# A decoder block on one core: the second channel product as seven block products on 2x2 blocks, left factors through DRAM

## The chip, the cores and the metric

The kernel runs on one core of a Trainium2 chip. A core has five engines that each work through their own instructions in order: TensorE (PE, matrix products into PSUM), VectorE (DVE), ScalarE (ACT), GpSimd (POOL) and SyncE (SP, which here only issues transfers). They wait for each other through semaphores. The metric is the device time of one execution in microseconds: 2101.83 us before the change, the median of three runs (2101.52 to 2101.94).

## The reference: what is computed

One decoder layer on 512 tokens of width 2048, all in float32: an input projection, eight heads of forgetting attention beside eight heads of spatial gating, an output projection with residual, and a channel MLP. The change is in the MLP and the norm behind it:

```
h2 = rmsnorm(x, norm_ffn_g)            # x: 512 x 2048
a = relu(h2 @ w_ff1)                   # first channel product, w_ff1: 2048 x 8192
x = x + (a * a) @ w_ff2                # second channel product, w_ff2: 8192 x 2048
return rmsnorm(x, norm_final_g)
```

## The kernel before, in words

Every large product is made of matmuls of 128x128 weights with 512 columns. To keep float32 accuracy each operand is split into two parts in the type fp32r (h = rounded, l = the rest), and `mm3` (L139) issues three matmuls: h by h, h by l and l by h.

The products are a list of units that `run_units` (L186) works through. A unit covers 512 output columns; each of its steps takes one weight tile of 128 rows by 512 columns and makes 12 matmuls on four PSUM banks. `prepare` (L190) runs three steps ahead: every second step it issues a load of two tiles (512 KB, `load_pair`, L156, on SP's queue), and `split_w` (L144) lets ACT make wh and DVE make wl, which are kept in four buffers of each.

The stream of the MLP goes in 16 parts of 512 hidden features. `f1_unit(u)` (L759) has 16 steps and makes part u of the first product, features on partitions, tokens on columns; `f1_done` (L617) scales by the norm's row rF and applies relu on DVE, squares on ACT, and splits the result into sh and sl, which stay in SBUF. `f2_unit(u)` (L762) follows one part behind: four units (g) of four steps, one for each 512 output columns, and `f2_done` (L629) adds the four banks into the running sum oa on DVE. So f and g alternate. The last part is `last_unit` (L639): by halves of 256 tokens, with matmuls of 256 columns (psl), and behind each half `last_norm` (L669) sums the squares, takes the root on POOL, spreads it over the partitions with a matmul and scales oa, which is stored to the output, features first.

The order on PE is the order of the program; the other engines' orders are made by a scheduler when the program is built. `tick` (L177) interleaves small tasks with the steps. PSUM has six banks for products (`mm`) and two more (`ax`).

## Time and profile before

| | |
|---|---|
| time, median of 3 runs | 2101.83 us |
| span of the profiled execution | 2100.5 us |
| time of a run outside such a span | about 1.3 us |
| PE busy | 2082.1 us (99%) |
| DVE busy | 1036.4 us (49%) |
| ACT busy | 740.7 us (35%) |
| POOL busy | 139.5 us (7%) |
| moved by DMA | 204.58 MB, mean 97 GB/s |

The page gives only the span of the profiled execution, from its first to its last instruction; what a run takes more than that is the difference of the first two rows. Busy time is the time in which an engine executes; a matmul's record is longer than the distance to the next, because matmuls are pipelined, so the pace is read from the starts. A wait that the page names with an arrow belongs to the engine that released it last.

### The profile page before, as it was taken

The numbers are of one execution on the slowest core, as the hardware profiler recorded it, in microseconds if no ns is written. First come the engines' busy times: TensorE is split into PE (matmuls) and PEld (weight loads), VectorE is DVE, ScalarE is ACT, GpSimd is POOL, SyncE is SP. The second block draws the span as 40 slices with busy tenths as digits, with TensorE's granted clock in tenths as the row PEclk, the third lists the DMA queues.
The fourth block names the chain that finished last, engine by engine and source line by source line (L and its number), as shares of the span: only waits on it lengthen the run. The fifth ranks groups of instructions, "written<-read, shape, count | busy, mean of one in ns | idle before, by whom it ended". The sixth has DMA issues, their size and how long they took to land.

```text
span 2100.5 us, 24282 instructions
## 1 busy us (share of the span) xinstructions
PE 2082.1 (99%) x9462; PEld 1728.6 (82%) x9462; DVE 1036.4 (49%) x1732; ACT 740.7 (35%) x1239; POOL 139.5 (7%) x123
## 2 busy tenths in 40 slices
PE   9999999999999999999999999999999999999997
PEld 6888888888888888888888888888888888888886
DVE  6466365575575644435334354343433434434465
...
DMA packets 60371, 204.58 MB, mean 97 GB/s; under 512 B 6496, under 2 KB 10720, under 8 KB 60128
## 3 DMA queue, kind: packets, MB, share of 16 engines
...
q8 instruction: 74, 1.21, 0.2%
...
q0 software_dynamic: 256, 0.52, 0.1%
...
## 4 chain that ended last, share of the span: by engine, by line
PE 97%; DVE 2%; issue 1%; ACT 0%; DMA 0%; SPq 0%; DVEq 0%; POOL 0%; ACTq 0%
PE ps_f L140 11%; PE ps_f L141 11%; PE ps_f L142 11%; PE ps_g L140 10%; PE ps_g L141 10%; PE ps_g L142 10%; PE ps_qk L140 3%; PE ps_qk L142 3%; PE ps_qk L141 3%; PE ps_zv L140 1%; PE ps_zv L142 1%; PE ps_zv L141 1%; PE ps_zu L142 1%; PE ps_zu L140 1%; PE ps_oa L141 1%; PE ps_oa L140 1%
## 5 line engine op out<-in xcount | busy, mean ns | idle before, releaser
L153 DVE SCALAR_TENSOR_TENSOR wl_f<-raw_f,cols,wh_f 128x512 fp32r<-128x512 f32 x256 | 193.1, 755 | 445.8 <-ACT wh_f L152 445.8
L140 PE MATMUL ps_f<-xh,wh_f 128*128 128x512 f32 x1024 | 398.5, 389 | 0.0
L142 PE MATMUL ps_f<-xh,wl_f 128*128 128x512 f32 x1024 | 398.4, 389 | 0.0
L141 PE MATMUL ps_f<-xl,wh_f 128*128 128x512 f32 x1024 | 398.4, 389 | 0.0
L140 PE MATMUL ps_g<-sh,wh_g 128*128 128x512 f32 x960 | 373.5, 389 | 0.0
L142 PE MATMUL ps_g<-sh,wl_g 128*128 128x512 f32 x960 | 373.5, 389 | 0.0
L141 PE MATMUL ps_g<-sl,wh_g 128*128 128x512 f32 x960 | 373.5, 389 | 0.0
L152 ACT ACTIVATE wh_f<-raw_f,cols 128x512 fp32r<-128x512 f32 x256 | 185.7, 726 | 494.4 <-PE ps_f L141 369.7
L149 DVE TENSOR_TENSOR wl_g<-raw_g,wh_g 128x512 fp32r<-128x512 f32 x240 | 165.4, 690 | 295.1 <-ACT wh_g L148 179.5
L148 ACT CAST wh_g<-raw_g 128x512 fp32r<-128x512 f32 x240 | 149.3, 622 | 405.8 <-PE ps_g L141 315.2
L140 PEld LDWEIGHTS ps_f<-xh,wh_f 128*128 128x128 f32 x1024 | 192.2, 188 | 39.9
L142 PEld LDWEIGHTS ps_f<-xh,wl_f 128*128 128x128 f32 x1024 | 192.2, 188 | 39.9
L141 PEld LDWEIGHTS ps_f<-xl,wh_f 128*128 128x128 f32 x1024 | 192.2, 188 | 39.9
L142 PEld LDWEIGHTS ps_g<-sh,wl_g 128*128 128x128 f32 x960 | 180.2, 188 | 37.4
L140 PEld LDWEIGHTS ps_g<-sh,wh_g 128*128 128x128 f32 x960 | 180.2, 188 | 37.4
L141 PEld LDWEIGHTS ps_g<-sl,wh_g 128*128 128x128 f32 x960 | 180.2, 188 | 37.4
L633 DVE TENSOR_TENSOR oa<-oa,ps_g 128x512 f32<-128x512 f32 x240 | 148.7, 680 | 7.4 <-PE ps_g L142 7.4
L140 PE MATMUL ps_qk<-xh,wh_qk 128*128 128x512 f32 x256 | 101.6, 397 | 0.0
L142 PE MATMUL ps_qk<-xh,wl_qk 128*128 128x512 f32 x256 | 100.0, 391 | 0.0
L141 PE MATMUL ps_qk<-xl,wh_qk 128*128 128x512 f32 x256 | 99.9, 390 | 0.0
L113 POOL TENSOR_TENSOR rt_last<-rt_last,neg_half 128x2 f32<-128x2 f32 x2 | 1.4, 697 | 1375.8 <-DVE rt_last L112 1375.8
L153 DVE SCALAR_TENSOR_TENSOR wl_qk<-raw_qk,cols,wh_qk 128x512 fp32r<-128x512 f32 x64 | 47.8, 750 | 69.8 <-ACT wh_qk L152 69.2
...
## 6 DMA issues: line engine op xcount, KB each, us to landing
raw_f<-in_w_dram SPq DMA_DIRECT2D x128, 512.0 KB, 3.5
raw_g<-in_w_dram SPq DMA_DIRECT2D x120, 512.0 KB, 3.5
raw_qk<-in_win_dram SPq DMA_DIRECT2D x32, 512.0 KB, 3.5
raw_zv<-in_win_dram SPq DMA_DIRECT2D x16, 512.0 KB, 3.5
raw_zu<-in_win_dram SPq DMA_DIRECT2D x16, 512.0 KB, 3.5
raw_oa<-in_wout_dram SPq DMA_DIRECT2D x16, 512.0 KB, 3.5
raw_og<-in_wout_dram SPq DMA_DIRECT2D x16, 512.0 KB, 3.5
raw_v<-in_win_dram SPq DMA_DIRECT2D x15, 512.0 KB, 3.5
```

The source lines that it names most:

```text
L113: nc.gpsimd.tensor_tensor(dst, dst, neg_half[:, 0:1].broadcast_to([P, m]), ALU.pow)
L140: nc.tensor.matmul(ps, lhsT=ah, rhs=bh, start=start, stop=False)
L141: nc.tensor.matmul(ps, lhsT=ah, rhs=bl, start=False, stop=False)
L142: nc.tensor.matmul(ps, lhsT=al, rhs=bh, start=False, stop=stop)
L148: nc.scalar.copy(wh, raw)
L149: nc.vector.tensor_tensor(wl, raw, f(wh), ALU.subtract)
L152: nc.scalar.activation(wh, raw, AF.Copy, scale=g)
L153: nc.vector.scalar_tensor_tensor(wl, raw, g, f(wh), ALU.mult, ALU.subtract)
L633: nc.vector.tensor_tensor(a, a, ps[m], ALU.add)
```

## The change

The second product no longer follows the first part by part: all 16 `f1_unit` run first, then `second_product` runs.

**Behind the output projection** the gain of the norm is put into xh and xl, so w_ff1 is only split (no gain), and the norm's scale is left out of the first product: its square r2, by token, is applied at the very end. `turn_x2` transposes the residual (64 transposes of 128x128) and stores it in DRAM as x2d.

**In the first product** `f1_done` makes relu and square on ACT. `factors_task` makes of each part's 512x512 result four blocks (two halves of the tokens, two halves of the hidden features) and of these seven left factors: A11, A12, A22 and the sums S1 to S4 (four POOL instructions). Each factor is split into h and l (7 casts on ACT, 7 subtractions on DVE) and stored in DRAM (`fac`, 3.67 MB for a part).

**In `second_product`** the output has tokens on partitions and stays in SBUF (acc). There are 16 units x = (kc, n): 1024 hidden features by 1024 output columns each. A unit takes four blocks B11, B12, B21, B22 of w_ff2, each in two pieces h of 256 rows, and makes seven products P1 to P7 in place of the eight that 2x2 blocks by 2x2 blocks take. A product and a piece h is a group of 12 matmuls: 14 groups a unit, 2688 matmuls in all. Right factors are B11, B21, B22 as they are, and three combinations made in place: raw(B11) = B12 - B11 and t2 = B22 - that on DVE (L739, L740), raw(B12) = B22 - B12 on POOL (L742), raw(B21) = B21 - t2 on DVE (L752). Each is split like before, now in pieces of 128x1024, by ACT (L749) and DVE (L750) into three buffers. The four output blocks of a unit are sums of products: some sums form in PSUM by further accumulation, and three times a unit (P2, P7, P3) `add_kept` adds the bank to acc on DVE and then, from the second kc on, a kept product s to acc on POOL (L783). In the last kc `settle` applies r2, adds x2d and squares; `finish` then makes the last norm for a half of the tokens, transposes back and stores.

```diff
+    dram = ctx.enter_context(tc.tile_pool(name="dram", bufs=1, space=bass.MemoryType.DRAM))
...
     def g_done(c):
...
-                nc.scalar.copy(xh[k], o)
-                nc.vector.tensor_tensor(xl[k], o, f(xh[k]), ALU.subtract)
+                nc.scalar.activation(xh[k], o, AF.Copy, scale=g)
+                nc.vector.scalar_tensor_tensor(xl[k], o, g, f(xh[k]), ALU.mult, ALU.subtract)
...
+            start_task(turn_x2(c), 6)
+    def turn_x2(c):
+        for m in range(4):
+            xt = t2(f"x2t{c}_{m}")
+            pt = ax(f"px{c}_{m}", m % 2)
+            for tb in range(NT):
+                nc.tensor.transpose(pt[:, tb * P:(tb + 1) * P], oa[c][:, m, tb * P:(tb + 1) * P], ident)
+            nc.scalar.copy(xt, pt)
+            nc.sync.dma_start(out=x2d[c][:, :, m * P:(m + 1) * P], in_=xt.rearrange("p (t c) -> p t c", c=P))
+            yield 2
     def norm2_task():
...
-        parts = spread_parts(r, "ffn")
-        yield 4
-        spread(rF, *parts, "ffn")
+        nc.vector.tensor_tensor(r2, r, r, ALU.mult)
...
-    def f1_done(u):
...
-    def f2_done(fb):
...
-    def last_unit():
...
-    def last_norm(half, squares, c, n):
...
-    def last_weights_task():
...
+    NF = 7
+    A11, A12, A22, S1, S2, S3, S4 = range(NF)
+    fac = [dram.tile([NF, P, 1024], F32, name=f"fac{u}") for u in range(NU)]
+    def f1_done(u):
+        def done(ps):
+            sq = s8(f"sq{u}")
+            for m in range(4):
+                nc.scalar.activation(sq[:, m, :], ps[m], AF.Relu)
+                nc.scalar.activation(sq[:, m, :], sq[:, m, :], AF.Square)
+            start_task(factors_task(u, sq))
+    def factors_task(u, sq):
+        def v(t):
+            return t.rearrange("p (j c) -> p j c", j=2)
+        a11, a21 = sq[:, 0:2, 0:256], sq[:, 0:2, 256:512]
+        a12, a22 = sq[:, 2:4, 0:256], sq[:, 2:4, 256:512]
+        s = s8(f"s{u}")
+        s1, s2, s3, s4 = (v(s[:, i, :]) for i in range(4))
+        form = [a11, a12, a22, s1, s2, s3, s4]
+        def put(i, n):
+            t = s8(f"fc{u}_{i}", F32R)
+            for k in range(n):
+                h, l = v(t[:, 2 * k, :]), v(t[:, 2 * k + 1, :])
+                nc.scalar.copy(h, form[i + k])
+                nc.vector.tensor_tensor(l, form[i + k], f(h), ALU.subtract)
+            nc.sync.dma_start(out=fac[u][i:i + n].rearrange("i p c -> p i c"),
+                              in_=f(t)[:, 0:2 * n, :].rearrange("p (i a) c -> p i (a c)", i=n))
+        nc.gpsimd.tensor_tensor(s1, a21, a22, ALU.add)
+        nc.gpsimd.tensor_tensor(s3, a11, a21, ALU.subtract)
+        yield 2
+        put(A11, 2)
+        yield 2
+        nc.gpsimd.tensor_tensor(s2, s1, a11, ALU.subtract)
+        nc.gpsimd.tensor_tensor(s4, a12, s2, ALU.subtract)
+        put(A22, 2)
+        yield 3
+        put(S2, 2)
+        yield 2
+        put(S4, 1)
+    def second_product():
...
+        y_pool = pool("y_pool", 6)
+        f_pool = pool("f_pool", NF)
+        raw2 = pool("raw2", 4)
+        tmp_pool = pool("tmp_pool", 1)
+        w2_pool = pool("w2_pool", 3)
...
+        P1, P2, P3, P4, P5, P6, P7 = range(1, 8)
+        left = {P1: A11, P2: A12, P3: S4, P4: A22, P5: S1, P6: S2, P7: S3}
+        usual = (P1, P2, P6, P5, P7, P3, P4)
+        final = (P1, P2, P5, P6, P3, P7, P4)
+        units2 = [(kc, n) for kc in range(NK) for n in range(2)]
...
+        def load_factor(kc, p):
+            if kc >= NK:
+                return
+            t = f_pool.tile([P, 2, 1024], F32R, tag="fac", name=f"fac{kc}_{p}")
+            for h in range(2):
+                nc.sync.dma_start(out=f(t)[:, h, :], in_=fac[2 * kc + h][left[p]])
+            facs[kc, p] = t
+        def prepare(i):
+            x, p, h = groups[i]
+            def raw(b):
+                return raws[x, b, h]
+            if (p == P6 and order_of(x) is usual) or (p == P5 and order_of(x) is final):
+                t2t = tmp_pool.tile([P, 1024], F32, tag=f"tmp{h}", name=f"tmp{x}_{h}")
+                nc.vector.tensor_tensor(raw(B11), raw(B12), raw(B11), ALU.subtract)
+                nc.vector.tensor_tensor(t2t, raw(B22), raw(B11), ALU.subtract)
+                raws[x, "t2", h] = t2t
+                nc.gpsimd.tensor_tensor(raw(B12), raw(B22), raw(B12), ALU.subtract)
+            src = {P1: B11, P2: B21, P3: B22, P4: B21, P5: B11, P6: "t2", P7: B12}[p]
+            s = raws[x, src, h]
+            wh = w2_pool.tile([P, 1024], F32R, tag="wh", name=f"wh{x}_{p}_{h}")
+            wl = w2_pool.tile([P, 1024], F32R, tag="wl", name=f"wl{x}_{p}_{h}")
+            nc.scalar.copy(wh, s)
+            nc.vector.tensor_tensor(wl, s, f(wh), ALU.subtract)
+            if p == P6:
+                nc.vector.tensor_tensor(raw(B21), raw(B21), raws[x, "t2", h], ALU.subtract)
+            ready[i] = wh, wl
+            freed = {P5: B11, P7: B12, P3: B22, P4: B21}.get(p)
+            if freed is not None:
+                nxt = {P5: B11, P7: B21, P3: B12, P4: B22}[p]
+                load(x + 1, nxt, h)
...
+        def add_kept(c, s, first, bank):
+            if first:
+                for t in range(2):
+                    nc.vector.tensor_tensor(acc[c][:, t, :], s[:, t, :], bank[t], ALU.add)
+            else:
+                take(bank, add_ps(c))
+                nc.gpsimd.tensor_tensor(acc[c], acc[c], s, ALU.add)
...
+        def settle(th, q, x2l):
+            a = acc[th, q]
+            for t in range(2):
+                tb = 2 * th + t
+                nc.vector.scalar_tensor_tensor(a[:, t, :], a[:, t, :], r2[:, tb:tb + 1], x2l[:, t, :],
+                                               ALU.mult, ALU.add)
+                nc.scalar.activation(x2l[:, t, :], a[:, t, :], AF.Square, accum_out=sums[:, tb, q:q + 1])
+
+        def finish(th):
+            tbs = slice(2 * th, 2 * th + 2)
+            r = rl[:, tbs]
+            nc.vector.tensor_reduce(r, sums[:, tbs, :], axis=AX.X, op=ALU.add)
+            inv_root(r, r, D, 2)
+            for q in range(4):
+                for t in range(2):
+                    e = nc.vector if t == 0 else nc.gpsimd
+                    e.tensor_scalar(acc[th, q][:, t, :], acc[th, q][:, t, :], rl[:, 2 * th + t:2 * th + t + 1], None, ALU.mult)
+            yield 3
...
+        for i, (x, p, h) in enumerate(groups):
+            while n_ready < len(groups) and n_ready <= i + 2:
+                prepare(n_ready)
+                n_ready += 1
+            kc, n = units2[x]
+            chain = {P1: "X", P6: "X", P7: "X", P4: "X", P2: "Y", P5: "Z", P3: "Z"}[p]
+            new = p in (P1, P2, P5)
+            if p == P4 and order_of(x) is final:
+                chain, new = "W", True
+            if h == 0 and new:
+                banks[chain] = [mm(f"b{chain}{x}_{t}") for t in range(2)]
+            wh, wl = ready.pop(i)
+            a = facs[kc, p]
+            for j in range(2):
+                for t in range(2):
+                    c = slice(j * 256 + t * P, j * 256 + (t + 1) * P)
+                    ah, al = a[:, h, c], a[:, h, 512 + j * 256 + t * P:512 + j * 256 + (t + 1) * P]
+                    bh, bl = wh[:, j * 512:(j + 1) * 512], wl[:, j * 512:(j + 1) * 512]
+                    start, stop = new and h == 0 and j == 0, h == 1 and j == 1
+                    for w, (l, r) in enumerate(((ah, bh), (ah, bl), (al, bh))):
+                        nc.tensor.matmul(banks[chain][t], lhsT=l, rhs=r, start=start and w == 0,
+                                         stop=stop and w == 2, skip_group_check=True)
+            if h == 1:
+                evacuate(x, p)
+                if n == 1:
+                    load_factor(kc + 1, p)
+            tick()
...
-    f1_unit(0)
-    for u in range(1, NU):
+    for u in range(NU):
         f1_unit(u)
-        if u < NU - 1:
-            f2_unit(u - 1)
...
-    start_task(last_weights_task())
-    f2_unit(NU - 2)
-    run_units()
-    last_unit()
+    while tasks:
+        tick()
+    early.close()
+    second_product()
```

On DVE, in the stretch of the second product where part 7 goes through columns 1 and 2, the order of before is (wl_g7_1_0 is the low part of step 0 of part 7, columns 1; ps_g the banks, oa the running sum):

```order
L149 TENSOR_TENSOR wl_g7_1_0_10561<-raw_g7_1_0_10558,wh_g7_1_0_10560 128x512
L149 TENSOR_TENSOR wl_g7_1_1_10577<-raw_g7_1_0_10558,wh_g7_1_1_10576 128x512
L149 TENSOR_TENSOR wl_g7_1_2_10595<-raw_g7_1_2_10592,wh_g7_1_2_10594 128x512
L633 TENSOR_TENSOR oa0_4495<-oa0_4495,ps_g7_0_0_10542 128x512
L633 TENSOR_TENSOR oa0_4495<-oa0_4495,ps_g7_0_1_10543 128x512
L633 TENSOR_TENSOR oa0_4495<-oa0_4495,ps_g7_0_2_10544 128x512
L633 TENSOR_TENSOR oa0_4495<-oa0_4495,ps_g7_0_3_10545 128x512
L149 TENSOR_TENSOR wl_g7_1_3_10615<-raw_g7_1_2_10592,wh_g7_1_3_10614 128x512
```

Now DVE's order at the head of unit 7 is this (wl7_1_0 is the low part for unit 7, product P1, piece 0; raw7_0_0 is block B11, raw7_1_0 B12, raw7_2_0 B21, raw7_3_0 B22, each of piece 0; bX6 is the bank of unit 6's P4):

```order
L750 TENSOR_TENSOR wl7_1_0_12878<-raw7_0_0_12723,wh7_1_0_12877 128x1024
L739 TENSOR_TENSOR raw7_0_0_12723<-raw7_1_0_12803,raw7_0_0_12723 128x1024
L740 TENSOR_TENSOR tmp7_0_12951<-raw7_3_0_12842,raw7_0_0_12723 128x1024
L750 TENSOR_TENSOR wl7_1_1_12894<-raw7_0_1_12741,wh7_1_1_12893 128x1024
L766 TENSOR_TENSOR acc10_10871<-acc10_10871,bX6_0_12639 128x512
L766 TENSOR_TENSOR acc10_10871<-acc10_10871,bX6_1_12640 128x512
L750 TENSOR_TENSOR wl7_2_0_12912<-raw7_2_0_12762,wh7_2_0_12911 128x1024
L739 TENSOR_TENSOR raw7_0_1_12741<-raw7_1_1_12821,raw7_0_1_12741 128x1024
L750 TENSOR_TENSOR wl7_2_1_12930<-raw7_2_1_12782,wh7_2_1_12929 128x1024
L752 TENSOR_TENSOR raw7_2_0_12762<-raw7_2_0_12762,tmp7_0_12951 128x1024
L740 TENSOR_TENSOR tmp7_1_12974<-raw7_3_1_12860,raw7_0_1_12741 128x1024
L750 TENSOR_TENSOR wl7_6_0_12956<-tmp7_0_12951,wh7_6_0_12955 128x1024
```

Behind these stand the second L752 and wl7_6_1; so 12 instructions with two operands in SBUF and two on a bank stand where, for as many groups of matmuls, six splits and eight bank sums stood before.

On POOL, between the norm of the MLP and the end, the order of before is (ssf: sum of squares; rt: the norm's root; rT: the root spread; oa: the output):

```order
L602 TENSOR_TENSOR ssf_4870<-ssf_4870,x2_15_5700 128x512
L113 TENSOR_TENSOR rt_ffn_5795<-rt_ffn_5795,neg_half_95 128x4
L113 TENSOR_TENSOR rt_last0_15462<-rt_last0_15462,neg_half_95 128x2
L691 TENSOR_TENSOR oa0_4495<-oa0_4495,rT0_15524 128x2x256
L691 TENSOR_TENSOR oa1_4708<-oa1_4708,rT0_15524 128x2x256
```

Now POOL has in every unit from the third on, here unit 6 and the start of unit 7 (acc: the sums in SBUF; k1, k5, k2: the kept products):

```order
L742 TENSOR_TENSOR raw6_1_0_12518<-raw6_3_0_12560,raw6_1_0_12518 128x1024
L742 TENSOR_TENSOR raw6_1_1_12536<-raw6_3_1_12578,raw6_1_1_12536 128x1024
L783 TENSOR_TENSOR acc00_10867<-acc00_10867,k1_6_12669 128x1024
L783 TENSOR_TENSOR acc11_10872<-acc11_10872,k5_6_12796 128x1024
L783 TENSOR_TENSOR acc01_10868<-acc01_10868,k2_6_12755 128x1024
L742 TENSOR_TENSOR raw7_1_0_12803<-raw7_3_0_12842,raw7_1_0_12803 128x1024
L742 TENSOR_TENSOR raw7_1_1_12821<-raw7_3_1_12860,raw7_1_1_12821 128x1024
```

POOL, which had nothing to do in the MLP but one small root, now has five instructions of 1024 elements a unit, all with two operands in SBUF.

On SP's queue, where the last part of the first product ends, the order of before is (raw_f15: tiles of w_ff1 for the last part; raw_g14, raw_last: tiles of w_ff2):

```order
L161 DMA raw_f15_12_14610<-in_w1_dram 128x1024
L161 DMA raw_f15_14_14644<-in_w1_dram 128x1024
L161 DMA raw_g14_0_0_14736<-in_w2_dram 128x1024
L161 DMA raw_g14_0_2_14746<-in_w2_dram 128x1024
L161 DMA raw_last0_0_14772<-in_w2_dram 128x1024
```

Now it is this (fc15: the last part's factors; x2l: the residual; fac0_1: the left factor of P1 for the first kc; raw0_0_1: B11, piece 1, of unit 0):

```order
L667 DMA fac15_189<-fc15_0_10818 128x2x1024
L667 DMA fac15_189<-fc15_2_10826 128x2x1024
L667 DMA fac15_189<-fc15_4_10832 128x2x1024
L667 DMA fac15_189<-fc15_6_10838 128x1024
L791 DMA x2l10_14970<-x2d0_170 128x1024
L791 DMA x2l02_15264<-x2d2_172 128x1024
L728 DMA fac0_1_10877<-fac0_174 128x1024
L728 DMA fac0_1_10877<-fac1_175 128x1024
L718 DMA raw0_0_1_10882<-in_w2_dram 128x1024
L728 DMA fac0_2_10884<-fac0_174 128x1024
L728 DMA fac0_2_10884<-fac1_175 128x1024
L718 DMA raw0_2_1_10889<-in_w2_dram 128x1024
```

The first left factor, which the second product's first matmul reads, stands behind the stores of the last part's factors.

## Rows read from the trace of the kernel before

**Rows 1.** The page: busy time by engine; the chain that ended last.
```profile
PE 2082.1 (99%) x9462; PEld 1728.6 (82%) x9462; DVE 1036.4 (49%) x1732; ACT 740.7 (35%) x1239; POOL 139.5 (7%) x123
...
PE 97%; DVE 2%; issue 1%; ACT 0%; DMA 0%; SPq 0%; DVEq 0%; POOL 0%; ACTq 0%
```

**Rows 2.** Stretches (us): busy by engine, granted clock, DMA share, GB/s; MLP.
```profile
800.00:2000.00 1200.00, 1200.00 (x5296) 993.71 (x5295) 513.51 (x775) 359.81 (x560) 0.00 (x0) 1.00 0.30 98
```

**Rows 3.** Timeline of DVE, second product: start us, us, instruction, [idle before <-releaser].
```profile
787.26 0.69 DVE L149 TENSOR_TENSOR wl_g<-raw_g,wh_g 128x512 fp32r<-128x512 f32 x1 [1.76 <-ACT wh_g L148]
789.99 0.69 DVE L149 TENSOR_TENSOR wl_g<-raw_g,wh_g 128x512 fp32r<-128x512 f32 x1 [2.03 <-ACT wh_g L148]
...
793.31 2.47 DVE L633 TENSOR_TENSOR oa<-oa,ps_g 128x512 f32<-128x512 f32 x4
```

**Rows 4.** Timeline of PE, end of the last part.
```profile
2082.23 0.28 PE L141 MATMUL psl<-sl,wh_last 128*128 128x256 f32 x1
2082.35 0.28 PE L142 MATMUL psl<-sh,wl_last 128*128 128x256 f32 x1
```

**Rows 5.** Timeline of DVE, output projection, 599 to 607 us.
```profile
599.23 2.39 DVE L596 TENSOR_TENSOR xl<-oa,xh 128x512 fp32r<-128x512 f32 x2
601.54 1.77 DVE L594 TENSOR_TENSOR oa<-oa,x 128x512 f32<-128x512 f32 x1
...
604.50 0.68 DVE L596 TENSOR_TENSOR xl<-oa,xh 128x512 fp32r<-128x512 f32 x1
605.10 1.77 DVE L594 TENSOR_TENSOR oa<-oa,x 128x512 f32<-128x512 f32 x1
```

**Rows 6.** Timeline of POOL, same stretch and 618 us.
```profile
599.44 3.32 POOL L602 TENSOR_TENSOR ssf<-ssf,x 128x512 f32<-128x512 f32 x2 [12.24 <-ACT x L601]
604.64 1.68 POOL L602 TENSOR_TENSOR ssf<-ssf,x 128x512 f32<-128x512 f32 x1 [1.88 <-ACT x L601]
...
618.75 1.29 POOL L582 TENSOR_TENSOR part<-part,xh 128x512 f32<-128x512 f32 x1 [8.80 <-DVE part L581]
```

**Rows 7.** Timeline of DVE at 618 us: one operand in PSUM.
```profile
617.98 2.48 DVE L581 TENSOR_TENSOR part<-ps_oa,rA 128x512 f32<-128x512 f32 x4
```

**Rows 8.** Groups by line and form: count, busy us, mean ns, idle before.
```profile
L148 ACT CAST wh_g<-raw_g 128x512 fp32r<-128x512 f32 x240 | 149.3, 622 | 405.8 <-PE ps_g L141 315.2 <-PE ps_f L141 90.5 <-DMA raw_g<-in_w_dram 0.2
...
L654 DVE TENSOR_TENSOR oa<-oa,psl 128x256 f32<-128x256 f32 x32 | 13.4, 418 | 5.5 <-PE psl L142 3.8
...
L661 ACT ACTIVATE sql<-oa 128x256 f32<-128x256 f32 x30 | 12.5, 418 | 18.2 <-DVE oa L654 18.2
...
L691 DVE TENSOR_TENSOR oa<-oa,pb_last 128x768 f32<-128x768 f32 x4 | 3.5, 948 | 1.7 <-ACT rT L685 1.7
...
L691 POOL TENSOR_TENSOR oa<-oa,rT 128x256 f32<-128x256 f32 x4 | 2.8, 728 | 2.3 <-ACT rT L685 2.3
```

**Rows 9.** Timeline of PE, four transposes between products.
```profile
487.08 0.60 PE L530 MATMUL pg<-ident,u 128*128 128x128 f32 x4
487.43 0.48 PE L140 MATMUL ps_zu<-wh_zu,xh 128*128 128x512 f32 x1
```

**Rows 10.** The page's DMA issues: count, KB each, us to landing.
```profile
raw_g<-in_w_dram SPq DMA_DIRECT2D x120, 512.0 KB, 3.5
```

**Rows 11.** Stretches, as in rows 2: the start and the end.
```profile
12.00:20.00 8.00, 6.90 (x30) 5.07 (x29) 8.00 (x8) 5.76 (x11) 7.10 (x6) 1.00 1.04 399
...
2080.00:2086.00 6.00, 3.06 (x24) 2.88 (x23) 3.77 (x10) 4.40 (x10) 0.00 (x0) 0.89 0.01 4
2086.00:2090.00 4.00, 2.33 (x9) 1.90 (x9) 0.64 (x3) 0.71 (x2) 0.70 (x1) 0.50 0.00 0
```

**Rows 12.** Timeline of PE at the start of the program.
```profile
1.26 5.05 PE L84 MATMUL pwarm<-warm 128*128 128x512 bf16 x12 [1.26 <-DVE warm L65]
...
13.73 0.50 PE L141 MATMUL ps_v<-wl_v,xh 128*128 128x512 f32 x1 [0.80 <-DVE wl_v L153]
```

More of the change, by code (lines that the diff above doesn't have):

```diff
@@ L1 @@
 import math
+from contextlib import ExitStack
 import concourse.bass as bass
@@ L37, in hybrid_block, with early_pool @@
     const = ctx.enter_context(tc.tile_pool(name="const", bufs=1))
[L38 removed]
+    sm = ctx.enter_context(tc.tile_pool(name="sm", bufs=4))
     raw_pool = ctx.enter_context(tc.tile_pool(name="raw_pool", bufs=4))
[L40 to L43 removed]
+    dram = ctx.enter_context(tc.tile_pool(name="dram", bufs=1, space=bass.MemoryType.DRAM))
+    early = ExitStack()
+    def early_pool(name, bufs):
+        return early.enter_context(tc.tile_pool(name=name, bufs=bufs, reuse_waits="tile"))
+    w_pool = early_pool("w_pool", 4)
+    xs_pool = early_pool("xs_pool", 32)
+    s8_pool = early_pool("s8_pool", 10)
+    t2_pool = early_pool("t2_pool", 8)
     ps_mm = ctx.enter_context(tc.tile_pool(name="ps_mm", bufs=6, space=bass.MemoryType.PSUM))
@@ L569, in hybrid_block @@
     ffn = {}
-    rF = const.tile([P, 512], F32, tag="rB", name="rF")
     part = {}
@@ L605, in g_done @@
         return done
+    r2 = const.tile([P, NT], F32, name="r2")
+    x2d = [dram.tile([P, NT, 512], F32, name=f"x2d{c}") for c in range(4)]
+    def turn_x2(c):
[7 more added lines that the diff above has]
+            yield 2
     def norm2_task():
@@ L666, in last_unit @@
         while tasks:
             tick()
-    def last_norm(half, squares, c, n):
-        nt = n // P
-        pr = ax(f"pr_last{half}", 0)
-        for j in range(nt):
-            for i, ss in enumerate(squares):
-                nc.tensor.matmul(pr[:, j:j + 1], lhsT=ss[:, j * P:(j + 1) * P], rhs=one_col,
-                                 start=(i == 0), stop=(i == 1))
-        r = sm.tile([P, NT], F32, tag="rt", name=f"rt_last{half}")[:, 0:nt]
-        inv_root(r, pr[:, 0:nt], D, nt)
-        dg = t2(f"dg_last{half}")[:, 0:n]
-        for j in range(nt):
-            nc.vector.tensor_scalar(dg[:, j * P:(j + 1) * P], ident, r[:, j:j + 1], None, ALU.mult)
-        yield 3
-        pb = ax(f"pb_last{half}", 1)[:, 0:n]
-        nc.tensor.matmul(pb, lhsT=f(ones_r), rhs=dg, start=True, stop=True)
-        rT = t2(f"rT{half}")[:, 0:n]
-        nc.scalar.copy(rT, pb)
-        for fb in range(4):
-            split = 3 if half else 2
-            for e, ms in ((nc.vector, slice(0, split)), (nc.gpsimd, slice(split, 4))):
-                a = oa[fb][:, ms, c]
-                row = pb if half and e is nc.vector else rT
-                e.tensor_tensor(a, a, row.unsqueeze(1).broadcast_to([P, ms.stop - ms.start, n]), ALU.mult)
-            parts = 2 if half and fb == 3 else 1
-            for i in range(parts):
-                w = 4 // parts
-                rows = slice(fb * 512 + i * w * P, fb * 512 + (i + 1) * w * P)
-                nc.sync.dma_start(out=out[rows, c].rearrange("(m p) c -> p m c", p=P),
-                                  in_=oa[fb][:, i * w:(i + 1) * w, c])
-            yield 2
@@ L700, in hybrid_block @@
-    last_w = {}
-    def last_weights_task():
-        for kp in range(2):
-            for fb in range(4):
-                raw = load_pair(w2[((NU - 1) * 4 + fb) * 2 + kp], f"last{fb}_{kp}")
-                for kk in range(2):
-                    last_w[fb, 2 * kp + kk] = split_w(raw[:, kk, :], None, f"last{fb}_{2 * kp + kk}",
-                                                      xs_pool, ("xs", "xs"))
-                yield 1
     def first_load(k):
@@ L759, in f1_unit @@
     def f1_unit(u):
-        unit(f"f{u}", w1, 8 * u, KT, G_FFN, xact, True, f1_done(u))
-    def f2_unit(u):
-        for fb in range(4):
-            unit(f"g{u}_{fb}", w2, (4 * u + fb) * 2, 4, None, s_act(u), True, f2_done(fb))
-    f1_unit(0)
-    for u in range(1, NU):
+        unit(f"f{u}", w1, 8 * u, KT, None, xact, True, f1_done(u))
+    for u in range(NU):
         f1_unit(u)
-        if u < NU - 1:
-            f2_unit(u - 1)
     start_task(attention_task())
     run_units()
-    start_task(last_weights_task())
-    f2_unit(NU - 2)
-    run_units()
-    last_unit()
+    while tasks:
+        tick()
+    early.close()
+    second_product()
 def _pieces(np, w):
```

160 lines of the change are left out of this document (115 added, 45 removed).

## The prediction, written before the run

> **What bounds the kernel now.** I read the page first, and of it the busy times and the chain: PE is busy 99% of the span and the chain that ended last lies 97% on PE [rows 1]. The stretches say the same of the channel product: from 800 to 2000 us PE never rests, its clock is granted whole, DVE has 43% and ACT 30% of the time, POOL nothing, and the DMA engines move 98 GB/s [rows 2]. 5296 matmuls in 1200 us are 0.2266 us each, so a group of 12 is 2.72 us, which is also the distance of two splits on DVE [rows 3]. Then I read DVE's and POOL's timelines where both work at once (rows 5 and 6), since that is what the change makes usual, the forms of different sizes for the slopes (rows 8), and the loads where many are in flight (rows 10 and 11). The span of the profiled execution and 1.3 us around it make 2101.8, the median of the runs, so I sum against that.
>
> **The matmuls.** Before: 15 parts of 192 matmuls at 0.2267 (2880, 652.8 us) and the last part's 384 of 256 columns, 0.12 from start to start [rows 4], 46.1 us. After: 16 units of 14 groups of 12, 2688, 609.3 us. Term: -89.6. The first product keeps its count, and 43.5 us of PE a part cover its new work: ACT 8 passes over banks and 7 casts of 512 beside 16 splits, some 19 us at 0.62; DVE 16 splits and 7 subtractions, 16 us at 0.68, and four POOL instructions, each of which holds DVE up by 1.1 (below); 3.67 MB of stores beside 4.2 MB of loads, 180 GB/s. I cost all that at nothing; without cover it would be DVE's 20 us a part. The spreading of the norm falls away, 0.4 us.
>
> **turn_x2.** Four transposes hold the next product back 0.35 us [rows 9], 64 of them 5.6 us. Term: +5.6.
>
> **The two-operand rule of DVE and POOL.** DVE's addition L594, 0.68 alone, takes 1.77 when a POOL addition starts beside it [rows 5, 6]: DVE stands still 1.09 for a POOL instruction of 512 elements, which takes 1.29 by itself and 1.68 where it has to wait itself [rows 6]. Where DVE reads a bank in PSUM beside POOL it loses nothing, 2.48 for four [rows 7]. So instructions of both engines with two operands in SBUF exclude each other. To size 1024 elements: DVE goes from 0.418 (256) to 0.948 (768) [rows 8], so about 1.21, and behind one another 0.60 for 512 (2.47 for four with the first at 0.68) [rows 3] gives 1.13. POOL goes from 0.728 (256) to 1.29 [rows 6, 8], so 2.41, and DVE loses about 2.2 to each. ACT goes from 0.418 to 0.622 [rows 8], so 1.03.
>
> **The junction.** The first matmul of the second product needs P1's factor of parts 0 and 1, stored long before, but its load stands on SP behind the last part's stores (the order shown), which wait for what follows the last product. After its last matmul: relu and square of the banks, about 3 us; on POOL S1, S3, S2, S4, in chain 1.29 each and held up by DVE, until about 8; S4's cast and subtraction until about 10.5. The first store goes out at about 6.6. A load needs 3.5 us to land [rows 10], 1.3 each if many are in flight at 399 GB/s [rows 11]: with seven pieces of 0.5 MB of stores, two x2 loads and the factor's first half, 6.6 + 2.2 + 10 x 1.3, PE starts about 22 us after its last product. Behind that 12 loads of 512 KB are due before raw(B22) of piece 1: about 16 us, and L740, L742, L752 and a split follow on it (1.13 + 2.2 + 2 x 1.13): 43 us, where PE would want them at 22 + 13.6 = 36. Another 7. Term: +29; from 15 (the queue lets the loads through as the data come) to 40.
>
> **The head of a unit.** The split of a group may begin when PE has done the group three before it (three buffers). Time 0 is the end of P3.1; PE does P4.0 and P4.1, then P1, P2 and P6, and the second matmul of P6.1 needs its low part at 5 x 2.72 + 5.44 + 0.2 = 19.2. DVE can start at about 1.4 (release and cast). Until then it has by the order shown 12 instructions of 1024 (13.6 us), the two bank sums (1.2) and three exclusions by POOL, L783 of P3 and two L742 (6.6): 21.4, done at 22.8. Late by 3.6 us; by 2.4 if the bank sums fall under an exclusion. I take 3.1 for units 3 to 14, 37 us, and 1.4 for units 1 and 2, where no L783 comes from the unit before, 3 us. Term: +40. Lower bound: what DVE needs in a whole unit, 20 x 1.13 + 8 x 0.60 + 5 x 2.2 = 38.4 against PE's 38.1, is 0.3 a unit, 4 in all. Upper: a POOL instruction that also waits out a DVE instruction, 1.13 more for one of the three, 4.4 a unit, 62.
>
> **The last kc.** settle adds 16 instructions of 512 with two SBUF operands and 16 squares. In unit 14 four of them fall into the head of the next: +2. Unit 15 has the head again (3.1) and its own settles and scalings on DVE and POOL in its second half, where 8 x 0.60 stand before splits: +4. Half of the last transposes lie in its stream, 32 x 0.09 = 2.9, and they wait for root and scaling, about 4. Term: +16, from 5 to 25.
>
> **The tail.** Before, 18.1 us from the last matmul's start [rows 4] to the end of the span. POOL's four scalings are now 512 wide (5.2 against 2.9 us), 8 transposes and one evacuation stand behind them, at half the clock, which the rows show granted 0.50 from 2086 on [rows 11], 8 x 0.18 + 0.68; sums over partitions and the spreading of the root go, 1.7. Term: +2.7, from -2 to +8.
>
> **Sum:** -89.6 + 5.6 + 29 + 40 + 16 + 2.7 - 0.4 = +3.3, so 2105 us. The likeliest case's own range, from its bounds with no more than two of them at an end, is 2088 to 2122.
>
> **Rivals.** *Exclusion absorbed.* The buffers and the slack at a unit's end take up the head: the limit is then the balance of a whole unit, 0.3 instead of 3.1. This decides if POOL's instructions fall into gaps of DVE or under bank sums; for it speaks that DVE's busy time alone (27 us a unit) is far below 38; against it that splits cannot run ahead over three buffers. 2105 - 36 = 2069: faster.
>
> *The queue is late.* An odd unit loads 8 blocks and 14 factor halves for the next kc, 22 x 512 KB = 11.5 MB in 41 us: 280 GB/s. At the start 399 went through in such pieces [rows 11], but of inputs alone, none just written, and it was for 8 us. Below 280 it decides: at 250 an odd unit takes 46 us, 7 x 4.9 = +34, 2139.
> The Trainium skill ("DMA: Bandwidth & Descriptors", Measured) asks for 1 MiB or more per transfer to reach three quarters of the peak, and its table gives 0.95 us for 64 KB and 6.15 for 1 MB; by a line between them a transfer of 512 KB would be an estimated 3.4 us, 155 GB/s, and 22 one behind the other 74 us a unit. That holds only without overlap, and the row with 399 GB/s speaks against it.
>
> *The clock falls.* If TensorE's clock drops in each stall of 2 to 4 us at the head, the next group of 12 runs at 1.2 GHz, 0.42 instead of 0.2267 us each as at the program's start (5.05 us for 12) [rows 12]: 2.4 us a unit, 14 times, +34, 2139. A stall of 0.80 us at 13.7 left the clock at 1.00 [rows 11, 12]; when PE had run out of work at the end it fell [rows 11], so a stall between those lengths is open.
> The Trainium skill ("TensorE: Matmul & The Clock Gate", A second HAM failure mode: psum-queue depth-cycling) reports a kernel whose short idle spells between groups of matmuls made the clock swing and cost throughput; no run here shows such spells yet.
>
> **How the numbers follow.** This measurement can tell a change of about 0.2%, 4 us. I give the forecast 0.48, of it 0.10 below 2098, 0.17 within 4 us and 0.21 above; the absorbed exclusion 0.25, all faster; the queue 0.14 and the clock 0.13, all slower. Faster 0.35, same 0.17, slower 0.48. The range runs from the absorbed case with a cheap junction, 2060, to the queue and the clock, 2142.
>
> **What the changed profile would show.** The first product ends as before, with PE at its pace; then a gap of some 22 us ahead of the first L910, ended by the load of fac0_1. Units repeat every 41.2 us, with idle time of PE ahead of P6 released by DVE's wl. L750 means about 1.6 us instead of 1.2, L742 and L783 2.4 or more, and the bank sums L766 stay at 0.6. In odd units the DMA moves about 280 GB/s and PE is not released by fac or raw; the clock stays at 1.00. I am wrong if the units repeat at 38.1 to 38.5 (the exclusion is absorbed), if PE waits on loads in odd units, if the clock falls within a unit, or if DVE's instructions do not lengthen beside POOL's.

## The result, and the profile after

The changed kernel takes 2128.55 us, median of 4 runs (2126.02 to 2129.65), against 2101.89 for the kernel before on the same chip: ratio 1.0126, 95% interval 1.0111 to 1.014. It is 1.3% slower. Forecast were 2105 and a range of 2060 to 2142, so the time lies in the range, 23.5 us above the forecast. The forecast's +3.3 us was less than the 4 us that the prediction could tell from nothing, so its sign says little. The waits are where they were forecast, but one term of the sum, the units, is half again as large as stated. The profiled execution has a span of 2126.2 us, 25.7 more than before.

The page shows where to look: 2688 matmuls in place of 3264 of the second product, but PE no longer at 99% [rows 1].

```profile
PE 2042.6 (96%) x8992; PEld 1674.0 (79%) x8992; DVE 1311.1 (62%) x1631; ACT 897.1 (42%) x1416; POOL 462.4 (22%) x261
```

PE's waits, in all, number of times, the longest:

```profile
PE bX L910 <- DVE wl L750: 31.4, 21, 2.6
PE bX L910 <- DMA fac<-fac: 22.9, 1, 22.9
PE pt L819 <- DVE acc L810: 7.4, 2, 3.7
PE bY L910 <- DVE wl L750: 6.5, 9, 1.6
```

Two things are waited for: the low parts that DVE makes, 30 times and never longer than 2.6 us, 37.9 us in all, and once the first left factor. On PE's timeline the borders of the stages are the last matmul of the first product, the first of the second, the first matmuls of P2 (tile bY) in units 1 and 15, and the last L910:

```profile
1389.31 0.39 PE L150 MATMUL ps_f<-xh,wl_f 128*128 128x512 f32 x1
1412.59 0.77 PE L910 MATMUL bX<-wh,fac 128*128 128x512 f32 x1 [22.89 <-DMA fac<-fac]
...
1464.14 0.39 PE L910 MATMUL bY<-wh,fac 128*128 128x512 f32 x1
...
2058.41 0.39 PE L910 MATMUL bY<-wh,fac 128*128 128x512 f32 x1
...
2106.97 0.40 PE L910 MATMUL bW<-wh,fac 128*128 128x512 f32 x1
```

Against PE's pace (0.2267 us a matmul, 38.08 a unit, 5.44 for P1) these give the terms:

| term | forecast | measured | working |
|---|---|---|---|
| matmuls | -89.6 | -89.6 | counts and pace as forecast |
| transposes of x2, spread of the norm | +5.2 | +5.8 | what is left of 25.7 |
| junction and unit 0 | +29 | +31.1 | 1464.14 - 1389.31 = 74.83; without a wait 0.23 + 38.08 + 5.44 |
| units 1 to 14, from P2 to P2 | +42 | +61.2 | 2058.41 - 1464.14 = 594.27; without a wait 14 x 38.08 = 533.1 |
| rest of unit 15 | +14 | +16.1 | 2106.97 - 2058.41 = 48.56; without a wait 143 x 0.2267 |
| tail | +2.7 | +1.1 | 2126.2 - 2106.97 = 19.2, before 18.1 |
| sum | +3.3 | +25.7 | |

So 19 of the 22 us that the forecast missed lie in the units. From unit 3 on they repeat in pairs; the stretches show an odd unit and a pair (columns as in [rows 2]):

```profile
1548.75:1587.35 38.60, 38.44 (x170) 31.45 (x168) 34.90 (x27) 17.77 (x20) 14.74 (x5) 1.00 0.78 299
1719.39:1804.69 85.30, 80.57 (x337) 65.02 (x336) 75.51 (x57) 35.72 (x40) 30.72 (x11) 0.96 0.50 185
```

Two units take 85.3 us, 42.65 each, where PE alone would need 38.08. The DMA moves 299 GB/s in the stretch in which the next factors are loaded, and PE waits for no load there. The clock is 0.96. PE waits in two places, in even units for the low part of P6's first piece, in odd units for that of P1's second piece. DVE's timeline at the head of unit 8, an even one, shows the first wait being made (P6's first low part is the last row):

```profile
1757.45 1.21 DVE L750 TENSOR_TENSOR wl<-raw,wh 128x1024 fp32r<-128x1024 f32 x1
1758.58 1.21 DVE L739 TENSOR_TENSOR raw<-raw,raw 128x1024 f32<-128x1024 f32 x1
1759.72 1.21 DVE L750 TENSOR_TENSOR wl<-raw,wh 128x1024 fp32r<-128x1024 f32 x1
1760.86 3.41 DVE L752 TENSOR_TENSOR raw<-raw,tmp 128x1024 f32<-128x1024 f32 x1
1764.19 1.21 DVE L740 TENSOR_TENSOR tmp<-raw,raw 128x1024 f32<-128x1024 f32 x1
1765.32 1.21 DVE L750 TENSOR_TENSOR wl<-tmp,wh 128x1024 fp32r<-128x1024 f32 x1
```

and POOL beside it:

```profile
1760.02 3.17 POOL L742 TENSOR_TENSOR raw<-raw,raw 128x1024 f32<-128x1024 f32 x1 [3.58 <-ACT wh L749]
```

L752 takes 3.41 instead of 1.21, 2.2 more: POOL's L742 began while DVE was at the instruction before. This is the pattern of [rows 5, 6] at twice the size. PE at the same place:

```profile
1764.08 0.39 PE L910 MATMUL bX<-wh,fac 128*128 128x512 f32 x1
1766.59 0.63 PE L910 MATMUL bX<-wl,fac 128*128 128x512 f32 x1 [2.12 <-DVE wl L750]
1767.02 1.05 PE L910 MATMUL bX<-wh,fac 128*128 128x512 f32 x2
```

It stands 2.12 us, and the matmuls behind are 0.43 apart, twice the usual distance. A stretch of 3 us there has the granted clock:

```profile
1767.00:1770.00 3.00, 3.00 (x8) 2.30 (x7) 3.00 (x5) 0.50 (x1) 0.00 (x0) 0.50 0.00 0
```

0.50 is 1.2 GHz. In unit 7, an odd one, P1's second piece waits. Its split L750 and the L739 two instructions before it both met POOL; P6's first low part comes later, at 1724.12 (PE, then DVE):

```profile
1704.33 0.39 PE L910 MATMUL bZ<-wh,fac 128*128 128x512 f32 x1
...
1715.17 0.50 PE L910 MATMUL bX<-wl,fac 128*128 128x512 f32 x1 [2.06 <-DVE wl L750]
```
```profile
1707.24 3.30 DVE L739 TENSOR_TENSOR raw<-raw,raw 128x1024 f32<-128x1024 f32 x1
...
1711.72 3.40 DVE L750 TENSOR_TENSOR wl<-raw,wh 128x1024 fp32r<-128x1024 f32 x1
...
1724.12 1.21 DVE L750 TENSOR_TENSOR wl<-tmp,wh 128x1024 fp32r<-128x1024 f32 x1
1725.26 1.21 DVE L752 TENSOR_TENSOR raw<-raw,tmp 128x1024 f32<-128x1024 f32 x1
```

The clock fell behind this stall too, and not behind those of 1.14 to 1.37 in units 1 and 2 (a stretch from 1468.4 to 1544 has 1.00). By the starts of the matmuls each fall costs PE 1.7 us. So of the 9.1 us that two units lose, PE stands still for 4.6 (2.06, 0.40 and 2.12) and loses 3.4 at half the clock; what makes up the other 1.1 is open. DVE's and POOL's groups of the second product (as in [rows 8]):

```profile
L750 DVE TENSOR_TENSOR wl<-raw,wh 128x1024 fp32r<-128x1024 f32 x192 | 297.3, 1560 | 98.1 <-ACT wh L749 98.1
L752 DVE TENSOR_TENSOR raw<-raw,tmp 128x1024 f32<-128x1024 f32 x32 | 65.2, 2041 | 0.1
L766 DVE TENSOR_TENSOR acc<-acc,bX 128x512 f32<-128x512 f32 x56 | 35.8, 678 | 0.0
...
L783 POOL TENSOR_TENSOR acc<-acc,k 128x1024 f32<-128x1024 f32 x42 | 124.5, 2965 | 309.3 <-DVE acc L766 304.4 <-DVE rl L120 4.9
L742 POOL TENSOR_TENSOR raw<-raw,raw 128x1024 f32<-128x1024 f32 x32 | 101.3, 3167 | 166.1 <-ACT wh L749 38.6 <-DMA raw<-in_w_dram 36.0 <-issue 34.6
```

The splits, alone 1.21, mean 1.56; the bank sums, with one operand in PSUM, stay at 0.68.

### The profile page after: what moved, and what is told of

Read it like the earlier page. It is cut to its first block, busy times and chain, and to the rows that moved or that the text cites. A ratio compares the mean times of both kernels' runs of the same rounds, so it can differ in the third digit from the quotient of the medians.

```text
span 2126.2 us, 24004 instructions
## 1 busy us (share of the span) xinstructions
PE 2042.6 (96%) x8992; PEld 1674.0 (79%) x8992; DVE 1311.1 (62%) x1631; ACT 897.1 (42%) x1416; POOL 462.4 (22%) x261
## 5 line engine op out<-in xcount | busy, mean ns | idle before, releaser
L157 DVE TENSOR_TENSOR wl_f<-raw_f,wh_f 128x512 fp32r<-128x512 f32 x256 | 186.8, 735 | 408.1 <-ACT wh_f L156 367.6
L910 PE MATMUL bX<-wh,fac 128*128 128x512 f32 x1008 | 336.9, 409 | 25.1 <-DMA fac<-fac 22.9
L750 DVE TENSOR_TENSOR wl<-raw,wh 128x1024 fp32r<-128x1024 f32 x192 | 297.3, 1560 | 98.1 <-ACT wh L749 98.1
L156 ACT CAST wh_f<-raw_f 128x512 fp32r<-128x512 f32 x256 | 159.7, 624 | 401.1 <-PE ps_f L149 391.8
L749 ACT CAST wh<-raw 128x1024 fp32r<-128x1024 f32 x192 | 201.7, 1053 | 240.0 <-PE bX L910 137.7
L910 PEld LDWEIGHTS bX<-wh,fac 128*128 128x128 f32 x1008 | 200.7, 199 | 69.1 <-issue 23.3
L910 PE MATMUL bX<-wl,fac 128*128 128x512 f32 x504 | 208.5, 414 | 31.7 <-DVE wl L750 31.4
L783 POOL TENSOR_TENSOR acc<-acc,k 128x1024 f32<-128x1024 f32 x42 | 124.5, 2965 | 309.3 <-DVE acc L766 304.4
L910 PE MATMUL bZ<-wh,fac 128*128 128x512 f32 x512 | 162.8, 389 | 0.0
L910 PEld LDWEIGHTS bX<-wl,fac 128*128 128x128 f32 x504 | 101.0, 200 | 63.0 <-DVE wl L750 41.6
L742 POOL TENSOR_TENSOR raw<-raw,raw 128x1024 f32<-128x1024 f32 x32 | 101.3, 3167 | 166.1 <-ACT wh L749 38.6
L910 PEld LDWEIGHTS bZ<-wh,fac 128*128 128x128 f32 x512 | 96.1, 188 | 20.0
L910 PE MATMUL bZ<-wl,fac 128*128 128x512 f32 x256 | 99.7, 389 | 0.5 <-DVE wl L750 0.5
```

Source lines behind the costliest of these rows:

```text
L156: nc.scalar.copy(wh, raw)
L157: nc.vector.tensor_tensor(wl, raw, f(wh), ALU.subtract)
L742: nc.gpsimd.tensor_tensor(raw(B12), raw(B22), raw(B12), ALU.subtract)
L749: nc.scalar.copy(wh, s)
L750: nc.vector.tensor_tensor(wl, s, f(wh), ALU.subtract)
L783: nc.gpsimd.tensor_tensor(acc[c], acc[c], s, ALU.add)
```

## The experiments

**POOL's work moved to DVE**, in part and whole. Edits, L742 and L783:

```
- nc.gpsimd.tensor_tensor(raw(B12), raw(B22), raw(B12), ALU.subtract)
+ nc.vector.tensor_tensor(raw(B12), raw(B22), raw(B12), ALU.subtract)     # d742, dboth
- nc.gpsimd.tensor_tensor(acc[c], acc[c], s, ALU.add)
+ nc.vector.tensor_tensor(acc[c], acc[c], s, ALU.add)                     # d783, dboth
```

> The two subtractions L742 of each unit run on DVE instead of POOL; the order on PE is the same. Theory E (DVE and POOL exclude each other where both read two operands from SBUF, and the head of a unit has three such exclusions): DVE gains 2 x 2.2 us of standing still and pays 2 x 1.13, so the head is 2.2 us shorter, which is the stall of 2.1 us that each unit has now; with the stall goes the half clock behind it (1.6 us a unit). Units 3 to 14 at 38.3 to 39.5 us instead of 42.65, in all 2075 to 2090 us. Rival W (DVE simply has too much of its own work at the head, POOL does not matter): two more instructions of 1.13 make the head longer, the stall 4.3 us, units about 45, in all 2155 to 2165.

2087.96 us, ratio to before 0.9934 (0.992 to 0.9949).

> The additions L783 of the kept products run on DVE instead of POOL, L742 stays on POOL. Theory E: one of the three exclusions at the head (2.2) becomes 1.13 of work, so the head gains 1.1 of its 2.1 us stall; the rest, about 1 us, may or may not bring the clock down (a stall of 1.1 to 1.4 in units 1 and 2 did not): units 39.2 to 41.5 instead of 42.65, in all 2085 to 2115. Rival W: 1.13 more at the head, 3.4 more in a unit: stall 3.2, in all 2140 to 2150.

2087.01 us, 0.9928 (0.9914 to 0.9943).

> L742 and L783 both on DVE; POOL has nothing left in the units until the last norm. Theory E: no exclusions; head 15 x 1.13 + 1.2 = 18.2 us from 1.4 on, done at 19.6 against 19.2: units 38.1 to 38.8, clock 1.00 throughout, DVE's L750 at 1.21 instead of 1.56 us mean. In all 2060 to 2075 us, faster than the kernel before. Rival W: DVE's own work grows by 5 x 1.13 in a unit, slower than now, 2150 or more.

2065.13 us, 0.9831 (0.9814 to 0.9847). Each edit gives DVE more instructions and makes the kernel 41 us faster; both together 63. Rival W falls three times. Two units in d742, in d783 and in dboth (three views):

```profile
1657.05:1736.82 79.77, 76.97 (x338) 62.84 (x337) 71.19 (x61) 35.52 (x41) 20.02 (x6) 1.00 0.56 197
```
```profile
1665.17:1744.29 79.12, 77.33 (x337) 62.77 (x336) 69.70 (x63) 35.52 (x41) 12.69 (x4) 1.00 0.55 199
```
```profile
1616.15:1693.52 77.37, 76.77 (x337) 62.91 (x336) 67.93 (x67) 35.73 (x41) 0.00 (x0) 1.00 0.57 204
```

DVE's busy time falls from 75.5 to 67.9 us though it does ten more instructions. In dboth its groups are back at the single duration, and the bank sums are what they were:

```profile
L750 DVE TENSOR_TENSOR wl<-raw,wh 128x1024 fp32r<-128x1024 f32 x192 | 232.9, 1219 | 93.0 <-ACT wh L749 93.0
...
L766 DVE TENSOR_TENSOR acc<-acc,bX 128x512 f32<-128x512 f32 x56 | 35.8, 679 | 0.0
```

The exclusion is thereby shown as the cause of the units' loss, together with the falls of the clock, which go with it: the stalls that d742 leaves, 1.37 to 1.44 us, leave the clock at 1.00. All three times lie in theory E's ranges; d742's units, 39.9 us, are 0.4 above theirs. The scheduler's order on DVE is not quite the same in the three runs, so the split between the two edits is rough.

**One more buffer.** `w2_pool` 4 instead of 3, `n_ready <= i + 3` instead of `i + 2`, `y_pool` 4.

> Four buffers of right factors instead of three and preparation three groups ahead instead of two, so DVE may start one group (2.72 us) earlier at the head of a unit; POOL's exclusions stay. (For the room the tiles for x2 and the output are four instead of six, which touches only the last kc.) Theory E (a burst at the head of the unit; over a whole unit DVE has room: 75.5 us busy of 85.3 in two units): the stalls of 2.1 us and the clock's fall go, units 38.1 to 39.5, in all 2065 to 2085. Rival B (over a whole unit DVE and POOL together are the bound, 38.4 and more against 38.1): units stay above 41, in all 2105 to 2128.

2101.83 us, 1.0001 (0.9992 to 1.0011): between the two, neither right. Two units:

```profile
1620.52:1702.39 81.87, 77.30 (x337) 62.90 (x336) 77.54 (x57) 35.34 (x41) 30.98 (x10) 1.00 0.53 193
```

The buffer takes 1.7 us off a unit, as much as a fall of the clock costs, and the clock stays whole. PE still stands 2.3 us at the head of each unit, now at P6's second piece: its L740 met L742 (3.4 us), ACT's cast waits for it, and PE for both. DVE is busy 77.5 of 81.9 us, standing still included. It has gaps left, so the bound of a whole unit is not reached; but 38.8 a unit is more than PE's 38.08, so more buffers alone could not hide all of it in this order.

**The clock.** In the odd units' P1 and the even units' P6 (fill8), or in P6 of all units and P1 of the odd ones (fillall), PE makes 8 matmuls into a spare bank behind the group's first matmul, `for _ in range(8): nc.tensor.matmul(spare, lhsT=ah, rhs=bh, start=True, stop=True)`.

> POOL's work as in the changed kernel; in units 3 to 14, between the first and the second matmul of the group where the longest stall of the unit falls (P1's second piece in odd units, P6's first in even ones), PE makes 8 matmuls whose result nobody reads, 1.8 us, a little under the stall of 2.06 to 2.13. They cannot shorten what PE waits for. Theory K (TensorE's clock falls to 1.2 GHz because PE stands still, and costs 1.6 us a unit behind each stall): the clock stays at 1.00, units 40.9 to 41.4 instead of 42.65, in all 2106 to 2114. Rival N (the slow matmuls behind the stall only fill time that DVE would take anyway, so the stall grows by as much): 2125 to 2133, no change.

2139.13 us, 1.0179 (1.0164 to 1.0194): slower than either. The stall was covered in P1, but in the odd units PE then stood about 3 us at P6, and the clock fell there in five of the six. In unit 13 the same stall left it at 1.00 (a stretch from 1991.6 to 1995), so the length of the stall does not decide alone.

> As fill8, with 8 idle-time matmuls in P6's first piece of every unit from 3 to 14, and in P1's second piece of the odd ones. In fill8 the clock no longer fell in the odd units' P1, but PE came to P6 earlier and waited 2.97 us there, with a fall behind it, once in two units. Theory K2 (what DVE delivers sets when PE may pass P6; a fall ahead of that wait costs nothing, a fall behind the last stall of a unit costs its 1.6 us): with P6 covered in every unit the last fall goes, two units take 84.5 to 85.3 instead of fill8's 86.6, in all 2125 to 2133. Rival N (the clock costs nothing anywhere, DVE takes the time): 2137 to 2143, as fill8.

2130.83 us, 1.0139 (1.0122 to 1.0155), as K2 said. Eight units of fill8 and of fillall (two views), and the same of the changed kernel:

```profile
1547.54:1896.27 348.73, 332.75 (x1409) 269.35 (x1408) 297.83 (x225) 142.88 (x161) 123.00 (x40) 0.97 0.52 181
```
```profile
1547.93:1887.91 339.98, 331.22 (x1441) 269.07 (x1440) 304.06 (x225) 142.91 (x161) 123.01 (x40) 1.00 0.52 186
```
```profile
1548.75:1889.99 341.24, 322.25 (x1345) 260.11 (x1344) 302.06 (x225) 142.88 (x160) 122.55 (x41) 0.96 0.50 185
```

Covering the last stall of the odd units as well gives 2.2 us for two units, with the same order on DVE in both runs, so a fall behind a unit's last stall does cost time. Yet the kernel with no fall at all takes 85.0 for two units and the one with both falls 85.3. The added matmuls are not the only difference: the scheduler's order on DVE changed with them. In the odd units of fill8 and fillall the second L752 stands ahead of the split for P6's first piece, so that low part comes 1.1 us later than in the order of the changed kernel (1724.12 and 1725.26 above); this is unit 7 of fillall:

```profile
1724.35 1.23 DVE L752 TENSOR_TENSOR raw<-raw,tmp 128x1024 f32<-128x1024 f32 x1
1725.50 2.35 DVE L750 TENSOR_TENSOR wl<-tmp,wh 128x1024 fp32r<-128x1024 f32 x2
```

Counted from the end of P3, the first matmul of P6 that needs a low part starts after 22.1 us in the odd units of fillall and after 20.8 in those of the changed kernel, after 19.5 in the even units of both. What fillall gains in an even unit, 1.7 us, it mostly loses again in the odd one. The near equality of 85.0 and 85.3 therefore does not show that the falls are free.

**The junction.** First the last part's stores were issued by ACT:

```
- nc.sync.dma_start(out=fac[u][i:i + n]...
+ (nc.scalar if u == NU - 1 else nc.sync).dma_start(out=fac[u][i:i + n]...
```

> The last part's four stores of factors are issued by ACT instead of SP; nothing else. Theory Q (the first factor's load stands in SP's order behind stores that wait for the last subtraction): the load is issued at once when the first product ends, the gap of 22.9 us ahead of the first L910 falls to 8 to 14; but the bytes due until product P6 of unit 0 are the same, so its wait (3.0 us now) grows by some of that; in all 2115 to 2126. Rival M (the load waits for the memory that the last part's tiles still hold): gap stays at 20 to 24 us, in all 2127 to 2130.

2126.48 us, 1.0117 (1.0102 to 1.0133): half right, the first gap as theory Q has it, the time 0.5 us above its range. The gap broke into pieces, on PE:

```profile
1402.42 0.80 PE L910 MATMUL bX<-wh,fac 128*128 128x512 f32 x1 [12.87 <-ACT wh L749]
...
1412.47 0.79 PE L910 MATMUL bX<-wh,fac 128*128 128x512 f32 x1 [4.68 <-ACT wh L749]
...
1429.76 0.50 PE L910 MATMUL bX<-wl,fac 128*128 128x512 f32 x1 [2.80 <-DVE wl L750]
```

SP now waited for memory: one wait of 10.4 us ahead of a factor's load and one of 6.8 ahead of a block's, both released by the stores of the last part. In jnp the pools of `second_product` were allocated in another order (f, raw2, tmp, w2, acc, s, y):

> Last part's stores issued by ACT as before in jn, and in addition the memory of the second product is laid out in another order, the tiles of left factors and weights first, so that they lie where the first product's activations were and not where the last part's factors wait for their stores. Theory QM (the start waits for the queue and, once that is free, for memory, as jn showed): the gap ahead of the first L910 falls from 22.9 to 8 to 14 us with no second gap of 4.7, loads run from the end of the first product on; in all 2108 to 2120. If the loads' bytes alone set the time of P6 in unit 0, P6 waits longer and it is 2122 to 2127.

2128.72 us, 1.0128 (1.0113 to 1.0143): no gain. ACT waited for the same stores, this time for the weights' tiles:

```profile
ACT wh L749 <- DMA fac<-fc: 14.7, 1, 14.7
```

The first matmul came later (1415.59), P6 of unit 0 waited less, and unit 1's P2 began at 1464.24 (1464.14 in the changed kernel). But the scheduler also moved loads: in jnp six of the 512 KB loads of x2 fall between 1385 and 1440, in the changed kernel two, in jn none. Four more are 5.3 us at the 393 GB/s of jnp's stretch from 1390 to 1430.

**Towards a faster kernel.** best: dboth and jnp together, and the scalings that `finish` gives to POOL (L810) on ACT.

> L742 and L783 on DVE, the stores and the memory as in jnp, and the last norm's scalings that POOL makes (1.72 us each of 512) on ACT. Sum: 2065 of dboth, 8 to 18 less at the start of the second product, 3 to 6 less at the end: 2042 to 2056. If the start is set by the bytes: 2058 to 2062.

2061.49 us, 0.9809 (0.9793 to 0.9826), the second case. best2: the last part's stores on POOL's queue, pools in the order f, raw2, tmp, s, acc, w2, y.

> As best, with the last part's stores issued by POOL, and the memory laid out so that the left factors, right factors and their raw tiles lie where nothing of the last part is kept; only the kept products and the sums lie there. Theory M (in best the start waits 26.4 us because the weights' tiles lie on the last part's factors, whose stores must have drained first): the first matmul starts 9 to 16 us after the first product instead of 26.4; the 10 loads that P6 needs come by about 1412, so 2042 to 2054 in all. Rival Y (the bytes set the time at which unit 0 ends, wherever memory lies): unit 1 begins at the same time as in best, 2058 to 2063.

2064.69 us, 0.9823 (0.9808 to 0.9837): theory M fails, the gap was 28.3 us, and P2 of unit 1 began at 1465.3 (best: 1461.9), so rival Y's range is missed by 1.7 us as well. best3: best2 with the fourth buffer.

> As best2, with four buffers of right factors and three groups of preparation ahead (kept products in three tiles, x2 in five). Without POOL in the units the stall of 0.3 us at P6's second piece (0.6 us a unit with the fill of the pipeline) should go: units 38.08 in place of 38.68, 6 to 8 us less than best2. If four buffers only move the wait (as they did beside POOL, 41.0 a unit): no less than best2.

2051.7 us, 0.9761 (0.9746 to 0.9775), 13 less than best2, more than expected. Its start and two units:

```profile
1390.00:1430.00 40.00, 20.34 (x60) 14.54 (x61) 21.21 (x20) 13.57 (x21) 8.44 (x8) 0.70 0.99 392
1538.00:1614.16 76.16, 76.16 (x337) 63.08 (x336) 67.58 (x67) 35.77 (x41) 0.00 (x0) 1.00 0.56 207
```

The units are at PE's pace, 38.08. At the start PE now begins 9 us after the first product, and yet P2 of unit 1 comes at 1461.84. So the bytes were left out:

```
+            if u == NU - 1: return        # no store
- in_=fac[2 * kc + h][left[p]]
+ in_=fac[min(2 * kc + h, NU - 2)][left[p]]
```

> best3 without the stores of the last part's factors (3.67 MB); where the last kc would read them it reads those of the part before, so that part of the result is left out, and the loads are as many. Theory Y (behind the first product the bytes queued there set when unit 0 ends; queue and memory only move the wait about): 3.67 MB at the 392 GB/s of that stretch are 9.4 us, so unit 1's product P2 begins at 1451 to 1455 instead of 1461.8, in all 2041 to 2046. Rival: the chain of the last part's factors through ACT, POOL and DVE sets it, 2049 to 2052.

2037.95 us, 0.9695 (0.9679 to 0.9712). The same stretch:

```profile
1390.00:1430.00 40.00, 28.20 (x110) 22.41 (x111) 31.36 (x29) 21.11 (x30) 5.71 (x4) 0.83 0.80 299
```

P2 of unit 1 begins at 1448.76, 13.1 us earlier, more than the 7 to 11 expected: without the stores the scheduler also put the loads of x2 (2.6 MB) later. In 40 us 12.0 instead of 15.7 MB were moved. The rival is refuted. For Y speaks that from 1390 to 1430 the DMA moved 389 to 393 GB/s at a share of 0.99 to 1.01 in jnp, best, best2 and best3, wherever the wait was named; there unit 0 ends when the bytes queued behind the first product are through. This run alone does not show it, since without the stores nothing holds the last part's memory either.

## Why the prediction was right or wrong

**Matmuls, transposes, first product, tail, unit 15** came out within 2.1 us a term; the first product kept PE's pace with its new work beside it.

**The junction** was right in size (31.1 against 29) and in the place of the gap (22.9 against 22). Its reason, SP's order, is shown in part only. With that order undone (jn) memory held the loads, with the memory moved (jnp) the weights' tiles waited for the same stores, and below lay the bytes. In the changed kernel itself the DMA's share was 0.33 from 1389.5 to 1400, and it was full only from then on. What the queue or the memory costs alone is not shown, since the runs that undid them also moved the loads of x2.

**The two-operand rule** was right: DVE stood still 2.0 to 2.2 us where it met a POOL instruction of 1024, as worked out from the smaller ones, and instructions on a bank did not. Over all, DVE's longer L739, L740, L750 and L752 come to 134 us for 74 POOL instructions, 1.8 each; some met a bank sum or a gap.
The Trainium skill ("SBUF — State Buffer", Who interferes with whom) says that a DVE instruction with two inputs in SBUF contends with a GpSimd instruction that reads SBUF, and that the order of issue decides who waits. The trace agrees, with 3.41 beside 1.21 us.

**The head of a unit** is the step that fell short, by its size: 61.2 against 42 with the settling of unit 14. Two things were mis-sized, the deadline and the clock.

The prediction checked one low part, that of P6's second piece, due at 19.2 us after the end of P3, and found it 3.6 late, taken as 3.1. The traces have it ready at 23.0 in odd and 21.8 in even units: 3.8 and 2.5 late, 3.2 on average, as forecast. But P6's first low part is missed by more. It is due at 5.44 + 4 x 2.72 + 0.2 = 16.5. By the order shown ten instructions of 1024, two bank sums and the same three exclusions stand up to it: 1.4 + 11.3 + 1.2 + 6.6 = 20.5, late by 4.0. Measured, its matmul starts at 20.8 in odd units, 4.3 late, and at 19.5 in even ones, 3.0 late, because there L740 stands behind the bank sums and loses 1.0 us instead of 2.2. In odd units PE takes half of that delay earlier, at P1's second piece, due at 5.44 + 2.72 + 0.2 = 8.4 with two exclusions ahead: 1.4 + 4 x 1.13 + 2 x 2.2 = 10.3 (it stood 2.06 us there). The numbers for both were there; the wrong deadline was checked. Of a burst's low parts the one that is missed by most sets the delay, here 3.6 on average.

The clock stood in the sum at nothing and beside it as a rival. It fell in every unit from 3 to 14. In odd units that adds nothing: PE, 1.7 us later at P6, still waits there for DVE. In even units no wait follows that could hide it, so 1.7 us come on top. Together (4.3 + 3.0 + 1.7) / 2 = 4.5 of the 4.57 that a unit lost, against 3.1: over twelve units some 10 us are the clock's and 6 the deadline's. This is read from the traces; no run takes the clock's falls away and leaves DVE's order as it is.

**The rival of the absorbed exclusion** (2069) is refuted even with a fourth buffer. Its balance, 38.4 a unit, was too low: in buf4 DVE was busy 38.8 of 40.9. **The late queue** is refuted: odd units moved 299 GB/s with no wait on a load.
The Trainium skill ("DMA: Bandwidth & Descriptors", Measured) asks for 1 MiB for three quarters of the peak; here pieces of 512 KB, many in flight, moved at 299 GB/s in an odd unit, which was all that was asked of them, and at 408 GB/s from 1420 to 1430, so that rule did not bite.
**The falling clock** happened as the rival described, behind stalls of 2.06 us and more. It took 1.7 us of PE instead of 2.4, and only in every second unit did that come on top.
